# The attention half's up-projection in seven-product units, its gate scaled earlier, the halves added in DRAM

## The chip, the cores and the metric

One core of a Trainium2 chip runs the whole kernel in one launch. The metric is device time in microseconds (us). The engines are TensorE (PE; its weight loads are PEld), VectorE (DVE), ScalarE (ACT), GpSimd (POOL) and SyncE (SP, which only issues DMAs here). Each engine works through its own queue in order.

## The reference, cut to what matters

The input is a residual stream x of 512 tokens by 2048 channels, and all arithmetic is float32.

```python
h = rmsnorm(x, attn_norm_g);  proj = h @ w_in        # u, v_sgu, q, k, v_att, g_a, g_b
y_a = chunked_spatial_gating(gelu(u), rmsnorm(gelu(v_sgu)))     # 512 x 1024
y_b = stick_breaking_attention(rmsnorm(q), rmsnorm(k), v_att)   # 512 x 1024
merged = sigmoid(g_a) * (y_a @ w_up_a) + sigmoid(g_b) * (y_b @ w_up_b)
x = x + merged @ w_o
x = x + (silu(gate) * up) @ w_ffn_out      # gate, up = rmsnorm(x) @ w_ffn_in
x = x + sigmoid(rmsnorm(x) @ w_ple_gate) * (p @ w_ple)
```

## The kernel before

Everything is kept transposed: channels lie on the 128 partitions, tokens along the free dimension. A **block** of an operand has 256 channels by 512 tokens (1024 columns of SBUF). A **pair** (`pair`, line 798) computes one block of 256 output channels. It consists of **units**, one for each 256 input channels.

A float32 product is made of three products of a high and a low part (`mm3`, line 287). A unit is of one of two kinds (`Pair.add`, line 648).

- Kind P, plain: 12 matmuls of 512 columns into two PSUM banks, y and z (lines 294 to 296).
- Kind S, Strassen's seven products on 256 x 256 quarters: undoubled it is 21 matmuls of 256 columns (lines 294 to 296) into four banks. Doubled, the high and low parts of the moving operand go through in one matmul of 512 columns (line 683). The quarters are put together by ACT and DVE in `mix` (lines 700 to 726) or `mix_doubled`.

Weights come two units at a time (a **double**). SP loads them into one of a few landing blocks, ACT splits off the high part (line 357) and DVE the low part (line 354). For an S double GpSimd also issues a DMA that adds two blocks onto the landed ones (line 361), and DVE makes two sums (line 373). There are three slots of split weights.

An operand is held as a **form**. A plain form (`plain_form`, line 604) is a block split into high and low. A late form (`late_form`, line 588) is what S units need: it loads a block, splits it (lines 284, 285) and can then serve as a plain operand. It later loads the same block again, the **second block**, and makes the other sums and splits of it (`plain_first`, line 525 for the sums). `until` says up to which pair j each unit still uses the plain operand, so that the first pairs of a stage are P while the second blocks are being worked on.

`tick()` (line 207) sets the order of this background work. It is called several times in each pair. It fetches a first block for one of the next three forms, builds the next form if its block has arrived and there is room, or else (`elif`) fetches one second block. A second block is held back as long as one of the next three forms of its stage has not been fetched. `after(n, fn)` puts work off by n ticks. Room comes from two arenas in SBUF: `parts` for forms, which has eight places for late forms, and `wholes` for raw blocks.

The stages in order are: the input projection with the attention and the spatial gating between its pairs (loop from line 1287), the **up stage** (loop from line 1338), the product with w_o (loop from line 1363), w_ffn_in, w_ffn_out in three passes, and the gate of the embeddings.

In the up stage j runs over eight output blocks, and for each j there is a pair "b" (y_b, attention) and then a pair "a" (y_a, spatial gating). All 16 pairs are PPPP. The gates' raw values were spilled to DRAM by the input projection. For each pair the gate block is loaded, DVE multiplies it by the row of the RMS norm (`scaled`, line 1209, 1212), ACT takes the sigmoid (line 1345), and DVE multiplies by the two banks (line 1350). After pair a, DVE adds the kept half b (line 1354), and one tick later SP stores the block `mix` (line 1332). The late forms of the w_o stage load it from there.

In the w_o stage the first pair (j = 0) is all P, the second is SSSSPPPP, the others are all S and doubled. At the end of a pair, `onto` adds the result to a block of x. Where a pair has both kinds, `rest` first takes in the banks y and z (line 787).

Of the kernel before, what the change touches and what calls it, by code (L numbers as in the profile page):

```python
# [31 lines left out]

PASSES = "SSSSSSSS", "SSSSSSSS", "SSSSPP"
# [35 lines left out]
def hybrid_layer(  # L69
# [137 lines left out]
    def tick():  # L207
# [396 lines left out]
    def plain_form(src, ready=always, gain=None, raw=1024, how="low", far=False):  # L604
        def steps(form):
            hi, lo = form.blocks = parts.take(1024, how), parts.take(1024, how)
# [16 lines left out]
        return Form("P", steps, [(parts, 1024, how)] * 2 + [(wholes, raw, "low")] * bool(raw),  # L623
# [555 lines left out]
    def sgu_v(rnd, o):  # L1179

        for h in range(2):
# [18 lines left out]
            for t in range(NT):  # L1200
# [7 lines left out]
                op0=ALU.mult, op1=ALU.add)  # L1208

# [70 lines left out]
    def y_form(c, i):  # L1280
        return plain_form((lambda: y_a[i]) if c == "a" else lambda: load(y_spill[i]),
                          lambda: len(y_done) == 8, raw=0 if c == "a" else 1024,
                          far=c == "b")

    ys = {(c, i): y_form(c, i) for c in "ba" for i in range(4)}
    build(ys.values())
    for n, ((w, i), pr) in enumerate(zip(order, made())):
# [25 lines left out]
        else:  # L1313
            d = tc.dram_tile([P, 1024], F32, name=nm("gsp"))
            nc.sync.dma_start(out=d, in_=o)
            gate_spill[w, i] = d
    finish_waiting()
    give(*att.values())


    part = {}
# [16 lines left out]
    for j in range(KU):  # L1338
        for b in "ba":
# [3 lines left out]
            def gate(g=g):  # L1343
                scaled(g, row1)
                nc.scalar.activation(g, g, AF.Sigmoid)

            after(1, gate)
            pr = pair([ys[b, i] for i in range(4)], last=j == KU - 1)
            for h, ps in zip((g[:, :T], g[:, T:]), pr.ends()):
                nc.vector.tensor_tensor(out=h, in0=h, in1=ps, op=ALU.mult)  # L1350
            if b == "b":
                part[j] = s
            else:
# [201 lines left out]
```

## Time and profile before

| | us |
|---|---|
| runs | 2667.51, 2673.37, 2673.16 (median 2673.16) |
| the profiled execution | 2668.2 |
| its span in the profile | 2666.5 |
| PE busy | 2640.4 |
| DVE busy | 2236.4 |
| ACT busy | 1413.9 |
| POOL busy | 453.4 |

The span is the time from the first to the last instruction of the program; the 1.7 us beside it lie around the program. Ends of matmuls are modelled, so PE's speed is read from the distance between starts, and from stretches with a known number of matmuls.

### The profile page before, as it was taken

How to read it: one execution, taken by the hardware profiler on the slowest of the kernel's cores; microseconds unless marked ns; L12 is line 12 of the kernel's file. 1: busy time of each engine (PE TensorE's matmuls, PEld its weight loads, DVE VectorE, ACT ScalarE, POOL GpSimd, SP SyncE). 2: the span in 40 equal slices, each digit the busy share in tenths (PEclk: the TensorE clock that was granted, in tenths of full speed). 3: DMA queues.
4: the chain of work that ended last, by engine and by line, in shares of the span. 5: the costliest groups of instructions: out<-in, count | busy, mean ns of one | idle time of the engine just before them, and what ended most of it. 6: DMA issues, size and time to landing. Idle time of an engine off the chain costs nothing.

```text
span 2666.5 us, 42598 instructions
## 1 busy us (share of the span) xinstructions
PE 2640.4 (99%) x15354; PEld 2312.4 (87%) x15354; DVE 2236.4 (84%) x3791; ACT 1413.9 (53%) x2245; POOL 453.4 (17%) x557
## 2 busy tenths in 40 slices
PE   8999999999999999999999999999999999999999
PEld 7888898888998888888888888888888888889898
DVE  8687878787887658989889888888889989989876
ACT  7656565655554334576444444444445445455643
POOL 0222322222220001101111111111110211211010
PEclk9999999999999999999999999999999999999999
DMA  7577777677775669988888878888787989988884
GB/s 227 158 190 174 185 173 187 171 182 197 179 188 186 214 212 264 239 265 223 220 218 207 210 194 207 203 203 202 197 209 223 263 220 277 226 248 246 252 229 134
DMA packets 293875, 560.16 MB, mean 210 GB/s; under 512 B 26400, under 2 KB 140832, under 8 KB 293664
## 3 DMA queue, kind: packets, MB, share of 16 engines
q1 hardware_dynamic: 231408, 442.08, 50.4%
q0 software_dynamic: 62256, 115.37, 27.0%
q8 instruction: 120, 1.97, 0.3%
q14 instruction: 91, 0.75, 0.1%
HBM read 505.97 MB, written 51.38 MB: 209 GB/s over the span
## 4 chain that ended last, share of the span: by engine, by line
PE 88%; DVE 5%; ACT 2%; DMA 2%; issue 1%; POOL 0%; SPq 0%; POOLq 0%; DVEq 0%; ACTq 0%
PE ps L683 49%; PE ps L295 10%; PE ps L296 10%; PE ps L294 10%; PE small L683 6%; DVE wlo L354 2%; DVE out L742 1%; PE small L1145 1%; PE small L1021 1%; DMA wholes<-x 1%; DMA wholes<-w_in 1%; ACT whi L357 1%; DVE wholes L373 0%; PE small L1095 0%; DVE parts L285 0%
## 5 line engine op out<-in xcount | busy, mean ns | idle before, releaser
L683 PE MATMUL ps<-parts,whi 128*128 128x512 f32 x4200 | 1404.7, 398 | 3.7 <-DVE out L787 3.1
L357 ACT ACTIVATE whi<-wholes 128x512 fp32r<-128x512 f32 (+3 forms) x941 | 872.5, 940 | 727.6 <-DVE wholes L373 270.5
L354 DVE TENSOR_TENSOR wlo<-wholes,whi 128x512 fp32r<-128x512 f32 (+3 forms) x941 | 982.7, 1079 | 65.8 <-ACT whi L357 64.0
L683 PEld LDWEIGHTS ps<-parts,wlo 128*128 128x128 f32 x4200 | 788.9, 188 | 178.4 <-DVE wlo L354 1.1
L683 PE MATMUL ps<-parts,wlo 128*128 128x256 f32 x4200 | 832.0, 279 | 0.0
L683 PEld LDWEIGHTS ps<-parts,whi 128*128 128x128 f32 x4200 | 676.4, 189 | 10.2 <-issue 4.5
L294 PE MATMUL ps<-parts,whi 128*128 128x256 f32 (+1 forms) x1822 | 598.9, 330 | 8.0 <-ACT parts L284 5.6
L295 PE MATMUL ps<-parts,whi 128*128 128x256 f32 (+1 forms) x1838 | 605.9, 330 | 0.8 <-DVE parts L285 0.8
L296 PE MATMUL ps<-parts,wlo 128*128 128x256 f32 (+1 forms) x1838 | 605.8, 330 | 0.0
L295 PEld LDWEIGHTS ps<-parts,whi 128*128 128x128 f32 x1838 | 348.4, 190 | 39.0 <-DVE parts L285 2.4
L294 PEld LDWEIGHTS ps<-parts,whi 128*128 128x128 f32 x1822 | 344.6, 190 | 41.5 <-ACT parts L284 6.7
L296 PEld LDWEIGHTS ps<-parts,wlo 128*128 128x128 f32 x1838 | 348.8, 190 | 30.8
L373 DVE TENSOR_TENSOR wholes<-wholes 128x256 f32<-128x256 f32 x822 | 345.1, 420 | 21.7 <-DMA wholes<-w_ffn_in 2.6
L742 DVE TENSOR_TENSOR out<-out,ps 128x256 f32<-128x256 f32 x490 | 202.9, 416 | 149.9 <-ACT out L739 149.4
L361 POOL DMA_DIRECT2D wholes<-w_ffn_in x170 | 148.0, 870 | 691.2 <-DVE wholes L373 197.4
L361 POOL DMA_DIRECT2D wholes<-w_in x132 | 116.3, 882 | 523.1 <-DMA wholes<-w_in 146.8
L683 PE MATMUL small<-parts,whi 128*128 128x512 f32 x480 | 190.3, 396 | 0.0
L285 DVE TENSOR_TENSOR parts<-wholes,parts 128x1024 fp32r<-128x1024 f32 (+3 forms) x148 | 138.1, 945 | 23.0 <-ACT parts L284 23.0
L284 ACT ACTIVATE parts<-wholes 128x1024 fp32r<-128x1024 f32 (+3 forms) x148 | 119.3, 830 | 55.1 <-DVE wholes L525 33.3
L739 ACT ACTIVATE out<-ps 128x256 f32<-128x256 f32 x258 | 95.7, 382 | 49.9 <-PE ps L683 46.4
L361 POOL DMA_DIRECT2D wholes<-w_ffn_out x64 | 55.6, 869 | 358.3 <-DMA wholes<-w_ffn_out 136.5
L1395 ACT ACTIVATE out<-out 128x512 f32<-128x512 f32 x44 | 27.9, 634 | 159.2 <-DVE out L1394 159.2
(123 smaller groups left out, 1750.2 us busy)
## 6 DMA issues: line engine op xcount, KB each, us to landing
wholes<-w_ffn_in SPq DMA_DIRECT2D x170, 384.0 KB, 5.6
wholes<-w_in SPq DMA_DIRECT2D x132, 384.0 KB, 5.0
wholes<-w_ffn_in SPq DMA_DIRECT2D x170, 256.0 KB, 4.8
wholes<-w_ffn_in POOLq DMA_DIRECT2D x170, 256.0 KB, 5.4
wholes<-w_in SPq DMA_DIRECT2D x132, 256.0 KB, 4.0
wholes<-w_in POOLq DMA_DIRECT2D x132, 256.0 KB, 5.0
wholes<-w_ffn_out SPq DMA_DIRECT2D x64, 384.0 KB, 6.3
wholes<-x SPq DMA_DIRECT2D x45, 512.0 KB, 5.6
```

The lines of the kernel that those rows point to most:

```text
L284: return (nc.scalar.activation(hi, src, AF.Copy), nc.vector.tensor_tensor(out=lo, in0=src, in1=hi.bitcast(F32), op=ALU.subtract))
L285: nc.vector.tensor_tensor(out=lo, in0=src, in1=hi.bitcast(F32), op=ALU.subtract))
L294: nc.tensor.matmul(ps, sh, mh, start=start, stop=False)
L295: nc.tensor.matmul(ps, sh, ml, start=False, stop=False)
L296: return nc.tensor.matmul(ps, sl, mh, start=False, stop=stop)
L354: in_turn(nc.vector.tensor_tensor(out=self.lo[:, blocks], in0=r, in1=h.bitcast(F32), op=ALU.subtract))
L357: in_turn(nc.scalar.activation(h, r, AF.Copy))
L361: nc.gpsimd.dma_start(out=raw[:, 3:5], in_=self.src[:, 1:3], accum_op=ALU.add)
L373: in_turn(nc.vector.tensor_tensor(out=o, in0=x, in1=y, op=ALU.add))
L683: m = nc.tensor.matmul(out, l, r, start=first and k == 0, stop=last and k == 1)
L739: in_turn(nc.scalar.activation(out, x, AF.Copy, scale=scale))
L742: in_turn(nc.vector.tensor_tensor(out=out, in0=x, in1=y, op=op))
```

## The change

- The pairs "a" and "b" change places: "a" comes first for each j.
- The forms of y_b become late forms. Pair b is PPPP for j = 0, SSPP for j = 1 and SSSS from j = 2 on (`UP_UNTIL`), undoubled, and ends with `mix` and one multiplication of 1024 columns.
- The gate block is multiplied by the norm's row in the input projection, two ticks after its pair, before it is spilled. The up stage only takes the sigmoid.
- The halves are no longer added by DVE. Pair a's product is stored by SP as `mix`, and pair b's product is added to it in DRAM by an accumulating DMA that GpSimd issues. Only then may the w_o stage load the block.
- `tick()` may fetch a second block in the same tick in which it builds a form, and also while first blocks are still to come, if `wholes` has room for these.
- In the w_o stage x's block is loaded at the start of its own pair, not a pair sooner. The norm's row and the attention's tiles are given back sooner. The first form of y_a takes its high part at the upper end of `parts`.

```diff
+UP_UNTIL = 1, 1, 2, 2
...
             builds.popleft().step()
-        elif seconds and fits([(wholes, 5 * 256, "old")]):
+        if seconds:
             f = (urgent or seconds)[0]
-            if f.used or not any(b.stage == f.stage and b.ready() and not b.there
-                                 for b in list(builds)[:AHEAD]):
+            first = [] if f.used else [b for b in list(builds)[:AHEAD]
+                                       if b.stage == f.stage and b.ready() and not b.there]
+            if fits([(wholes, 5 * 256, "old")] + [(wholes, 1024, "old") for _ in first]):
                 f.fetch_second()
...
+        if rnd == 3:
+            assert ("b", 3) in y_done
+            give(*att.values())
+            att.clear()
...
-            for b in "ba":
-                plan((w_up_a if b == "a" else w_up_b)[j], "PPPP")
+            for b in "ab":
+                plan((w_up_a if b == "a" else w_up_b)[j],
+                     "PPPP" if b == "a" else now("SSSS", UP_UNTIL, j))
...
+        if c == "a":
+            return plain_form(lambda: y_a[i], ready, raw=0, how="low" if i else ("high", "low"))
+        return late_form(lambda size=1024: load(y_spill[i], size), ready, far=True)
...
+            def spill_gate(o=o, d=d):
+                scaled(o, row1)
+                nc.sync.dma_start(out=d, in_=o)
+
+            after(2, spill_gate)
...
-            def gate(g=g):
-                scaled(g, row1)
-                nc.scalar.activation(g, g, AF.Sigmoid)
-
-            after(1, gate)
-            pr = pair([ys[b, i] for i in range(4)], last=j == KU - 1)
-            for h, ps in zip((g[:, :T], g[:, T:]), pr.ends()):
-                nc.vector.tensor_tensor(out=h, in0=h, in1=ps, op=ALU.mult)
-            if b == "b":
-                part[j] = s
+            after(1, lambda g=g: nc.scalar.activation(g, g, AF.Sigmoid))
+            pr = pair([ys[b, i] for i in range(4)], last=j == KU - 1, j=j,
+                      until=UP_UNTIL if b == "b" else None)
+            if pr.n["S"]:
+                tt(g, g, pr.out(), ALU.mult)
             else:
-                nc.vector.tensor_tensor(out=g, in0=g, in1=part[j].f(), op=ALU.add)
-                give(part.pop(j))
-                after(1, lambda j=j, s=s: store("mix", j, s))
+                for h, ps in zip((g[:, :T], g[:, T:]), pr.ends()):
+                    tt(h, h, ps, ALU.mult)
+
+            def store_merged(b=b, j=j, s=s):
+                if b == "a":
+                    nc.sync.dma_start(out=spill["mix", j], in_=s.f())
+                else:
+                    nc.gpsimd.dma_start(out=spill["mix", j], in_=s.f(), accum_op=ALU.add)
+                    there.add(("mix", j))
+                give(s)
+
+            after(1, store_merged)
...
-        if j < KU - 1:
-            raw.append(load(xT[j + 1]))
+        h = load(xT[j])
```

More of the change, by code (lines that the diff above doesn't have):

```diff
@@ L604, in plain_form @@
     def plain_form(src, ready=always, gain=None, raw=1024, how="low", far=False):
+        hows = [how] * 2 if isinstance(how, str) else how
         def steps(form):
-            hi, lo = form.blocks = parts.take(1024, how), parts.take(1024, how)
+            hi, lo = form.blocks = [parts.take(1024, h) for h in hows]
             w = form.raw()
@@ L621, in steps @@
             yield
-        return Form("P", steps, [(parts, 1024, how)] * 2 + [(wholes, raw, "low")] * bool(raw),
+        return Form("P", steps, [(parts, 1024, h) for h in hows] + [(wholes, raw, "low")] * bool(raw),
                     ready, src, far)
@@ L1280, in y_form, with ready @@
     def y_form(c, i):
[L1281 to L1285, printed above, removed]
+        def ready():
+            return len(y_done) == 8
+        if c == "a":
+            return plain_form(lambda: y_a[i], ready, raw=0, how="low" if i else ("high", "low"))
+        return late_form(lambda size=1024: load(y_spill[i], size), ready, far=True)
+    ys = {(c, i): y_form(c, i) for c in "ab" for i in range(4)}
     build(ys.values())
```

13 lines of the change are left out of this document (3 added, 10 removed).

## The prediction

> **What bounds the kernel now.** I read the page first, then the busy times by stage, then the rows of PE at the stage borders.
>
> ```profile
> span 2666.5 us, 42598 instructions
> PE 2640.4 (99%) x15354; PEld 2312.4 (87%) x15354; DVE 2236.4 (84%) x3791; ACT 1413.9 (53%) x2245; POOL 453.4 (17%) x557
> ```
>
> Busy times by stage (window; its length; PE, PEld, DVE, ACT, POOL busy; granted clock; DMA share; GB/s): input projection, up stage, start of w_o, most of w_ffn_in.
>
> ```profile
> 114.00:820.00 706.00, 698.21 (x4461) 623.12 (x4460) 576.31 (x1016) 423.37 (x868) 180.39 (x243) 1.00 0.72 182
> 820.00:995.00 175.00, 174.26 (x770) 143.53 (x769) 108.15 (x118) 64.36 (x63) 0.88 (x1) 1.00 0.61 205
> 995.00:1050.00 55.00, 51.91 (x277) 44.78 (x276) 44.34 (x74) 25.23 (x33) 6.94 (x8) 0.99 0.89 258
> 1190.00:1850.00 660.00, 659.51 (x3781) 575.41 (x3780) 589.94 (x1057) 329.32 (x460) 115.72 (x133) 1.00 0.82 211
> ```
>
> The reader is to see that PE is the bound nearly everywhere: in w_ffn_in it idles 0.5 us of 660 while DVE is busy 89%. In the up stage it idles 0.7 us, with DVE at 62%. So work taken from DVE there gives nothing by itself. Time can only come from fewer or shorter matmuls, or from the few places where PE stands. The change touches two such places. The first is early in the up stage:
>
> ```profile
> 832.10 0.73 PE L294 MATMUL ps<-parts,whi 128*128 128x512 f32 x2 [0.21 <-ACT parts L284]
> 833.36 0.50 PE L295 MATMUL ps<-parts,whi 128*128 128x512 f32 x1 [0.52 <-DVE parts L285]
> ```
>
> Here PE waits 0.21 and 0.52 us for the split of the y forms. The second is in w_o:
>
> ```profile
> 1043.65 0.63 PE L683 MATMUL ps<-parts,whi 128*128 128x512 f32 x2
> 1047.37 0.47 PE L683 MATMUL ps<-parts,whi 128*128 128x512 f32 x1 [3.09 <-DVE out L787]
> ...
> 1049.01 0.63 PE L683 MATMUL ps<-parts,wlo 128*128 128x256 f32 x2
> ```
>
> ```profile
> 1041.00:1043.90 2.90, 2.90 (x19) 2.49 (x17) 2.90 (x10) 1.08 (x2) 0.00 (x0) 1.00 1.08 232
> 1043.90:1047.40 3.50, 0.41 (x3) 0.06 (x1) 3.50 (x5) 1.00 (x3) 0.89 (x1) 1.00 0.91 331
> 1048.60:1052.10 3.50, 3.50 (x14) 3.02 (x13) 3.19 (x6) 2.74 (x3) 0.88 (x1) 0.51 1.00 277
> ```
>
> PE stands 3.1 us because `rest` (L787) of the second w_o pair is late on a DVE that is busy without a break. Then PE's granted clock is 0.51 for 3.5 us, which loses another 1.7 us. Both together are about 4.9 us, the largest single loss that I found in the trace.
>
> The Trainium skill bears on that price: "TensorE: Matmul & The Clock Gate", section "HAM oscillation — how this bites in real kernels", asks for no idle gaps of PE over about 3.4 us. By that rule 3.1 us would have stayed free of the half clock and the place would cost 3.1. The trace differs: 3.1 us of idleness was enough.
>
> **The matmuls.** One P unit runs from one start to the next start of the following unit; four undoubled S units fill a window of their own:
>
> ```profile
> 1015.28 0.39 PE L294 MATMUL ps<-parts,whi 128*128 128x512 f32 x1
> ...
> 1018.00 0.28 PE L294 MATMUL ps<-parts,whi 128*128 128x256 f32 x1
> ```
>
> ```profile
> 1018.00:1028.07 10.07, 10.07 (x85) 10.06 (x84) 9.07 (x15) 6.31 (x8) 0.89 (x1) 1.00 0.85 212
> ```
>
> A P unit takes 1018.00 - 1015.28 = 2.72 us. An S unit takes 10.07 / 4 = 2.518 us (84 matmuls of 0.12 us). The seven products save an eighth of the columns, but a 256-column matmul is a little dearer per column, so a unit saves 0.20 us, or 7.4%. S units are 2 in pair j = 1 and 4 in each of j = 2 to 7: 26. **26 x 0.204 = 5.3 us** on PE, the bound. This is the surest term.
>
> **DVE in the up stage.** Prices are from before's groups:
>
> ```profile
> L354 DVE TENSOR_TENSOR wlo<-wholes,whi 128x1280 fp32r<-128x1280 f32 x26 | 38.6, 1486 | 5.2 <-ACT whi L357 5.2
> L354 DVE TENSOR_TENSOR wlo<-wholes,whi 128x512 fp32r<-128x512 f32 x26 | 17.8, 684 | 3.8 <-ACT whi L357 3.8
> L373 DVE TENSOR_TENSOR wholes<-wholes 128x256 f32<-128x256 f32 x50 | 21.0, 420 | 2.3 <-DMA wholes<-w_ffn_out 1.6
> ```
>
> ```profile
> L354 DVE TENSOR_TENSOR wlo<-wholes,whi 128x1024 fp32r<-128x1024 f32 x33 | 40.3, 1222 | 12.9 <-ACT whi L357 12.9
> L1350 DVE TENSOR_TENSOR wholes<-wholes,ps 128x512 f32<-128x512 f32 x30 | 20.2, 686 | 18.1 <-PE ps L296 17.2 <-ACT wholes L1345 1.0
> L1212 DVE TENSOR_TENSOR wholes<-wholes 128x1024 f32<-128x1024 f32 x16 | 19.6, 1223 | 26.1 <-DMA wholes<-gsp 26.1
> L1354 DVE TENSOR_TENSOR wholes<-wholes 128x1024 f32<-128x1024 f32 x7 | 8.6, 1225 | 0.2
> L284 ACT ACTIVATE parts<-wholes 128x1024 fp32r<-128x1024 f32 x11 | 11.4, 1051 | 14.0 <-DMA wholes<-mix 8.3 <-DMA wholes<-y 5.6
> L285 DVE TENSOR_TENSOR parts<-wholes,parts 128x768 fp32r<-128x768 f32 x3 | 2.9, 952 | 0.0
> ```
>
> Removed: 16 scalings, 19.6 us, and 8 additions of halves, 9.8 us. Added: an S double costs DVE 1.49 + 0.68 + 2 x 0.42 = 3.01 instead of 1.22, so 13 doubles cost 23.3 more. Six `mix` cost 5 x 0.42 + 0.69 = 2.8 each, 16.8, and that of j = 1 costs 3.1. The second blocks of four y_b forms cost 4 x 0.42 + 0.95 = 2.6 each, 10.5. Sum: 108.2 - 29.4 + 53.7, about 132 of 170 us, or 78%. That is below the 89% at which w_ffn_in loses nothing, so I cost it at nothing. Its cover is thin in one place: a pair b of S units needs 6.0 + 2.8 + 1.2 = 10.0 us of DVE in 10.07 us of PE. The pair a beside it needs only 3.8 in 10.9, and split weights are one double (5 us) ahead.
>
> **The start of the up stage.** In before the y_b blocks must come from DRAM in the last pair of the projection. With y_a first, the forms needed first are already in SBUF, and y_b has one pair more. I take the 0.7 us above as gone (bounds 0 and 0.7).
>
> **The gate's scaling in the projection.** 16 operations of 1.22 us go onto DVE, which goes there from 576 to 596 of 706 us. They are put off two ticks, and behind each on DVE stand the steps of the attention, for which PE waits at places like this:
>
> ```profile
> 288.98 1.42 PE L1145 MATMUL small<-wholes 128*128 128x512 f32 x3 [0.84 <-ACT wholes L1138]
> ```
>
> From below, nothing excludes a loss of 0. From above, each of some 12 gates beside the attention delays PE by 0.4 us, 5 us in all. I take **1.5 us** lost, nearer to 0, since most of that DVE's work isn't waited for. The buffer of the gate is used again only two pairs later, and its store moves with it.
>
> **The halves added by DMA.** Half b no longer goes through DVE but through a GpSimd DMA, and the load of the merged block waits on SP until that has landed. The same form of DMA stands in w_ffn_out (issues: KB each, median us from issue to landing; then its minimum, median and maximum):
>
> ```profile
> x<-out POOLq DMA_DIRECT2D x16, 512.0 KB, 8.9
> wholes<-mix SPq DMA_DIRECT2D x16, 512.0 KB, 5.5
> ```
>
> ```profile
> DMA to landing us min/median/max: 5.0/8.9/9.7
> ```
>
> For blocks 0 to 6 there are a pair or more of time, and nothing is lost. SP stands some 5 us longer per block, and behind the load stand weights (a slot and a landing ahead, over 10 us) and the next gate block, whose sigmoid ACT can wait for at 37% busy. Block 7 is the last operand of the first w_o pair. Before:
>
> ```profile
> 998.41 0.33 SPq L1332 DMA_DIRECT2D mix<-wholes  x1
> ...
> 1001.83 0.33 SPq L516 DMA_DIRECT2D wholes<-mix  x1
> ```
>
> ```profile
> 1010.41 1.22 DVE L285 TENSOR_TENSOR parts<-wholes,parts 128x1024 fp32r<-128x1024 f32 x1
> ```
>
> ```profile
> 1000.38 0.87 POOL L361 DMA_DIRECT2D wholes<-w_o  x1 [6.37 <-DMA wholes<-w_o]
> ```
>
> Store at 998.4, load at 1001.8, split done by 1011.6, and needed at 1015.28, the start of the last unit: 3.7 us to spare. By durations alone the split could end at 1001.83 + 5.5 + 1.05 (ACT, L284) + 1.22 = 1009.6, so 5.7 to spare. The adding DMA takes 8.9 where the store took 3.4, 5.5 more: 0.2 to spare. It can also stand on POOL behind a w_o weight's addition that starts at 1000.38 and takes 0.87 (2.8 us), and behind a DVE that is up to 2 us late after an S pair. Bounds: 0 (landing in 5.0 us) and 4.6 of standing plus 1.7 of half clock, 6.3. I take **2.0 us** lost.
>
> **Second blocks sooner.** Busy time of DVE in the sums of second blocks (L525) around the start of w_o:
>
> ```profile
> 860.00:920.00 60.00, 4.54 (x12) 1.00 0.58 192
> 920.00:995.00 75.00, 0.00 (x0) 1.00 0.63 214
> 995.00:1015.00 20.00, 0.00 (x0) 1.00 0.90 277
> 1015.00:1050.00 35.00, 7.64 (x19) 0.98 0.88 248
> ```
>
> Three forms get their second blocks in the up stage (12 operations), none from 920 to 1015, and five crowd behind 1015. These are what makes L787 late. Fetching in the same tick as a build brings them forward into DVE's idle time. Against it: late forms of y_b take more of `parts` than plain ones, so only two merged forms fit beside them, not three. One more second block, 2.6 us of DVE, comes to this place; and loads behind block 7's stand on SP until its addition has landed. Bounds: nothing and the whole 4.9 us. I take **3.5 us** won.
>
> x's block in w_o is loaded a pair later but 20 us before its use, against the 5.5 us that a load of this size takes in the row of mix above: nothing. In the other stages PE hardly stands, so sooner second blocks give nothing there.
>
> **Sum.** -5.3 - 0.7 + 1.5 + 2.0 - 3.5 = -6.0 us. On the profiled execution, 2668.2, that is 2662.2. The shown runs lie at 2667.5 and at 2673.2 and 2673.4, so the profiled one is of the lower kind and 5 us under the median. I take the middle of the two kinds, 2670.5, and forecast **2664.5 us**.
>
> **The rivals.**
>
> 1. Everything hides: block 7 in time, the 4.9 us wholly gone, the scaling free: -5.3 - 0.7 - 4.9 = -10.9, 2659.6. For it: 7.6 us of idle DVE between 995 and 1018. Against it: the tight block 7.
> 2. Block 7 late at its upper bound and the stall at 1044 still there, since second blocks queue behind it on SP: -5.3 - 0.7 + 1.5 + 6.3 = +1.8, 2672. For it: 8.9 against 3.4 us. Against it: 5.7 us to spare.
> 3. Slower: DVE becomes the bound of the S pairs. From j = 2 on it needs 10.0 of 10.07 us and in some of them a merged form as well (1.22 + 2.6). If PE then waits for split weights 3.7 us in each of six pairs, that is +22 - 6 = +16, 2686. It decides from the point where DVE's backlog passes the 5 us that weights are ahead. 3.8 doesn't, and pair a pays it back, so I hold it unlikely.
> 4. The change doesn't do what it says: no room in `wholes`, second blocks come when they came. Then -6.0 + 3.5 = -2.5, 2668.
>
> **How the numbers follow.** Chances: forecast 0.45, rival 1 0.18, rival 2 0.17, rival 3 0.10, rival 4 0.10. Against the median of 2673.16, 0.3%, about what a measurement can tell from no change, is 8 us, so faster means under 2665.1. Rival 1 and half of the forecast lie there: 0.40. Slower is rival 3 and a little of rival 2: 0.12. The rest is 0.48. The range reaches from rival 1 on a run of the lower kind, 2668.2 - 10.9 = 2657, to rival 2 with the scaling at 5 us on a run of the upper kind, 2673.2 + 5.3 = 2678. It leaves out rival 3.
>
> **What would show it.** The up stage 6 us shorter with PE idle under 1 us in it; no stall at L787 in the second w_o pair, or a shorter one, with no half clock; a wait of the last unit of the first w_o pair for L285 or L284 of 0 to 4 us; L525 busy between 995 and 1015; losses of PE in the projection up by 1 or 2 us. A wait of PE for L354 in the S pairs would prove rival 3.

## The result and the profile after

The changed kernel is slower: 2681.36 us (median of 6 runs, 2679.03 to 2686.46) against 2669.97 us for the kernel before on the same chip (6 runs, 2667.51 to 2673.37). The ratio is 1.0043, interval 1.0033 to 1.0053. That is some 11 us, and 3 us above the upper end of the range. The profiled execution took 2680.76 us, 12.6 more than that of before.

Line numbers below are those of the changed kernel unless a listing is of another: the three matmuls of a unit are L296 to L298, the doubled ones L687, the splits of forms L286 and L287, those of weights L359 and L356, GpSimd's addition of weights L363, DVE's sums L375, sums of second blocks L527 (the same helper line also holds the multiplications by the gate now), every plain load L518, `rest` L791, the sigmoid L1357, the store of pair a's product L1368, the addition of pair b's L1370. The page begins:

```profile
span 2678.6 us, 43332 instructions
PE 2640.7 (99%) x15589; PEld 2321.8 (87%) x15589; DVE 2268.5 (85%) x3893; ACT 1436.2 (54%) x2286; POOL 466.2 (17%) x578
```

The same four windows as before, with the columns of the prediction:

```profile
114.00:820.00 706.00, 701.02 (x4468) 625.31 (x4468) 594.92 (x1036) 429.25 (x871) 173.94 (x242) 1.00 0.73 185
820.00:995.00 175.00, 170.10 (x998) 151.40 (x997) 113.58 (x171) 74.25 (x88) 17.66 (x20) 0.98 0.86 250
995.00:1050.00 55.00, 48.17 (x242) 40.37 (x240) 48.39 (x80) 27.46 (x37) 7.09 (x9) 0.94 0.89 265
1190.00:1850.00 660.00, 656.12 (x3745) 571.61 (x3744) 583.94 (x1046) 327.65 (x457) 115.00 (x132) 1.00 0.83 209
```

The projection is no worse. PE now stands 4.9 us in the up stage (0.7 before), 6.8 in the start of w_o (3.1) and 3.9 in the window of w_ffn_in (0.5). In the up stage and w_o the granted clock is lower too, and the DMA share of the up stage went from 0.61 to 0.86. I follow the first stall backwards. PE, then DVE, ACT, SP and POOL (start, length, engine, line, idle time before and what ended it):

```profile
907.62 0.39 PE L297 MATMUL ps<-parts,whi 128*128 128x512 f32 x1
912.91 0.79 PE L298 MATMUL ps<-parts,wlo 128*128 128x512 f32 x1 [4.90 <-DVE wlo L356]
```

```profile
911.29 0.42 DVE L713 TENSOR_TENSOR out<-out 128x256 f32<-128x256 f32 x1 [11.26 <-ACT out L710]
911.64 1.22 DVE L356 TENSOR_TENSOR wlo<-wholes,whi 128x1024 fp32r<-128x1024 f32 x1
```

```profile
909.72 1.06 ACT L1357 ACTIVATE wholes<-wholes 128x1024 f32<-128x1024 f32 x1 [11.86 <-DMA wholes<-gsp]
910.68 1.07 ACT L710 ACTIVATE out<-ps 128x512 f32<-128x512 f32 x2
```

```profile
901.17 0.33 SPq L518 DMA_DIRECT2D wholes<-mix  x1
901.54 0.43 SPq L518 DMA_DIRECT2D wholes<-gsp  x1
```

```profile
894.02 0.89 POOL L1370 DMA_DIRECT2D mix<-wholes  x1 [7.74 <-DVE wholes L527]
```

The reader is to see one queue after another stop behind a DMA. GpSimd issues the addition of a block at 894.02. SP's next instruction loads that merged block, so SP stands until the addition has landed, at 901.15. Behind it in SP's queue is the next gate block, issued at 901.54 and landed at 909.70. ACT's next instruction is that block's sigmoid: ACT idles 11.86 us, 3.7 of them before the load is issued and 8.2 while it is under way. The copies of `mix` (L710) behind it could have run: the last matmul of their S pair starts at 901.81. DVE idles 11.26 us behind those copies, and the low part of the weights that PE wants comes after them. PE's row names DVE L356 as the releaser, but DVE was not busy, it was waiting. Then the clock is low (window 910.60 to 917.40):

```profile
910.60:917.40 6.80, 4.49 (x11) 3.52 (x12) 5.93 (x11) 2.55 (x5) 0.29 (x1) 0.50 0.51 175
```

This stall costs 5.1 us of standing and 2.2 of half clock, 7.3 in all, found from the starts. It is the deepest of a kind, as the waits in 840 to 1010 us show (engine, line, what it waited for: us in total, times, longest). The changed kernel's ACT and SP:

```profile
ACT wholes L1357 <- DMA wholes<-gsp: 46.3, 12, 11.9
ACT whi L359 <- DMA wholes<-w_up_b: 12.1, 3, 5.6
...
SPq L518 <- DMA mix<-wholes: 75.7, 13, 8.9
```

SP in the kernel before, same window:

```profile
SPq L516 <- DVE wholes L1354: 24.6, 7, 4.9
...
SPq L516 <- DMA mix<-wholes: 15.9, 8, 2.2
```

The second place is the start of w_o:

```profile
1006.42 0.50 PE L297 MATMUL ps<-parts,whi 128*128 128x512 f32 x1 [1.96 <-DVE parts L287]
...
1016.49 1.43 PE L296 MATMUL ps<-parts,whi 128*128 128x512 f32 x3 [4.25 <-ACT parts L286]
```

```profile
1002.22 0.87 POOL L363 DMA_DIRECT2D wholes<-w_o  x1 [5.77 <-DMA wholes<-w_o]
1002.85 1.16 POOL L1370 DMA_DIRECT2D mix<-wholes  x1
```

```profile
1011.75 1.28 SPq L518 DMA_DIRECT2D wholes<-mix  x3
...
1015.38 1.06 ACT L286 ACTIVATE parts<-wholes 128x1024 fp32r<-128x1024 f32 x1 [7.19 <-DMA wholes<-mix]
```

Block 7's addition starts at 1002.85 (its store started at 998.41 before) behind a w_o weight on POOL. SP can load the block at 1011.75, ACT splits it at 1015.38, and PE has stood 4.25 us. With a smaller wait before it, a later one of 0.6 us and a half clock from 1016.4 to 1023.2, PE loses 10.8 us here. The kernel before lost 4.9 here, in its stall at L787, which is absent now. The third place is the border to w_ffn_in:

```profile
1203.18 0.86 PE L296 MATMUL ps<-parts,whi 128*128 128x512 f32 x3 [2.78 <-ACT parts L286]
```

```profile
1204.10:1207.50 3.40, 3.40 (x13) 2.92 (x12) 3.40 (x9) 3.04 (x6) 1.03 (x2) 0.51 0.99 225
```

By stages, from the ends of the same operations in both traces, the changed kernel is 2.8 us behind at the end of w_o's seventh pair, loses 5.5 more by early w_ffn_in, 0.1 in the rest of that stage, 2.6 by the end of the first 14 pairs of w_ffn_out and 1.3 in what follows. So some 9 of the 12 us in the profiled executions are lost behind w_o's seventh pair.

### The profile page after: what moved, and what is told of

Its sections match the earlier page's. It is cut to its first block, busy times and chain, and to the rows that moved or that the text cites. A ratio compares the mean times of both kernels' runs of the same rounds, so it can differ in the third digit from the quotient of the medians.

```text
span 2678.6 us, 43332 instructions
## 1 busy us (share of the span) xinstructions
PE 2640.7 (99%) x15589; PEld 2321.8 (87%) x15589; DVE 2268.5 (85%) x3893; ACT 1436.2 (54%) x2286; POOL 466.2 (17%) x578
## 5 line engine op out<-in xcount | busy, mean ns | idle before, releaser
L687 PE MATMUL ps<-parts,whi 128*128 128x512 f32 x4200 | 1404.0, 398 | 2.2 <-DVE out L746 1.0
L359 ACT ACTIVATE whi<-wholes 128x512 fp32r<-128x512 f32 (+2 forms) x954 | 882.9, 939 | 715.5 <-DVE wholes L375 306.5
L356 DVE TENSOR_TENSOR wlo<-wholes,whi 128x512 fp32r<-128x512 f32 (+2 forms) x954 | 992.1, 1074 | 40.1 <-ACT whi L359 39.7
L687 PEld LDWEIGHTS ps<-parts,wlo 128*128 128x128 f32 x4200 | 789.0, 188 | 179.0 <-issue 1.9
L687 PE MATMUL ps<-parts,wlo 128*128 128x256 f32 x4200 | 832.7, 279 | 0.0
L687 PEld LDWEIGHTS ps<-parts,whi 128*128 128x128 f32 x4200 | 675.4, 189 | 10.3 <-issue 4.4
L298 PE MATMUL ps<-parts,wlo 128*128 128x256 f32 (+1 forms) x1916 | 619.0, 324 | 6.7 <-DVE wlo L356 6.7
L297 PE MATMUL ps<-parts,whi 128*128 128x256 f32 (+1 forms) x1916 | 619.7, 324 | 5.8 <-DVE parts L287 5.8
L296 PE MATMUL ps<-parts,whi 128*128 128x256 f32 (+1 forms) x1899 | 611.2, 323 | 14.0 <-ACT parts L286 12.1
L297 PEld LDWEIGHTS ps<-parts,whi 128*128 128x128 f32 x1916 | 365.1, 191 | 41.4 <-DVE parts L287 8.6
L296 PEld LDWEIGHTS ps<-parts,whi 128*128 128x128 f32 x1899 | 362.0, 191 | 43.3 <-ACT parts L286 12.7
L298 PEld LDWEIGHTS ps<-parts,wlo 128*128 128x128 f32 x1916 | 365.4, 191 | 35.7 <-DVE wlo L356 8.3
L375 DVE TENSOR_TENSOR wholes<-wholes 128x256 f32<-128x256 f32 (+1 forms) x848 | 355.0, 419 | 28.3 <-DMA wholes<-w_ffn_in 4.5
L363 POOL DMA_DIRECT2D wholes<-w_ffn_in x170 | 148.2, 871 | 698.5 <-DVE wholes L375 225.4
L363 POOL DMA_DIRECT2D wholes<-w_in x132 | 116.0, 879 | 532.2 <-DMA wholes<-w_in 144.1
L687 PE MATMUL small<-parts,whi 128*128 128x512 f32 x480 | 190.4, 397 | 0.0
L287 DVE TENSOR_TENSOR parts<-wholes,parts 128x1024 fp32r<-128x1024 f32 (+3 forms) x162 | 144.0, 900 | 28.6 <-ACT parts L286 28.5
L286 ACT ACTIVATE parts<-wholes 128x1024 fp32r<-128x1024 f32 (+3 forms) x162 | 124.9, 795 | 60.5 <-DVE wholes L527 34.2
L363 POOL DMA_DIRECT2D wholes<-w_ffn_out x64 | 55.7, 871 | 354.4 <-DMA wholes<-w_ffn_out 135.7
```

The source lines that it names most:

```text
L286: return (nc.scalar.activation(hi, src, AF.Copy), nc.vector.tensor_tensor(out=lo, in0=src, in1=hi.bitcast(F32), op=ALU.subtract))
L287: nc.vector.tensor_tensor(out=lo, in0=src, in1=hi.bitcast(F32), op=ALU.subtract))
L296: nc.tensor.matmul(ps, sh, mh, start=start, stop=False)
L297: nc.tensor.matmul(ps, sh, ml, start=False, stop=False)
L298: return nc.tensor.matmul(ps, sl, mh, start=False, stop=stop)
L356: in_turn(nc.vector.tensor_tensor(out=self.lo[:, blocks], in0=r, in1=h.bitcast(F32), op=ALU.subtract))
```

## The experiments

Each ratio is to the kernel before in runs on the same chip, in five rounds. The profiled execution of one kernel can lie 3 us or more off its median, so medians carry the verdicts and traces the causes. In the changed kernel the last gate block is scaled after the place of the norm's row has been handed on. In e4 that place is overwritten by then, so there the block is scaled by other data. From e5 on (not in e15) the row is kept three ticks longer.

**e1: the old rule for second blocks, alone.**

```diff
-        if seconds:
+        elif seconds and fits([(wholes, 5 * 256, "old")]):
```

> The changed kernel with the old rule for second blocks (one piece of background work a tick, held back while a first block is to come). Theory A: the new rule itself costs the stalls at the start of w_ffn_in (span 1200, 5.4 us with the half clock) and at the start of w_ffn_out (span 2059, 3 us), because second blocks get in front of the last first block; with the old rule both go, and the span falls from 2678.6 by 8 to 12 us. Rival B: these stalls come from what the earlier stages hand over late, not from the rule; then they stay and the span falls by less than 2 us.

1.0037 [1.0024, 1.0049]. The up stage still has a stall (4.7 us at 887.7, ended by a split of weights) and ACT still waits 44.2 us for gate blocks. At the border the stall stays, though it comes 9 us later. So the rule by itself isn't the cause, as rival B had it.

**e2: the new rule alone, in the kernel before** (the same lines the other way round).

> The kernel before with the new rule for second blocks and nothing else. Theory A: +5.4 and +3 us at the two later stage borders, and at most 4.9 us won at span 1044: 2666.5 becomes 2668 to 2675. Rival B: no loss at the borders, 4.9 us won: 2662.

1.0024 [1.0015, 1.0033]. The part that I priced at -3.5 us costs 6 by itself. The stall at L787 is gone from the trace, but PE stands 3.1 us at 1013.3 for the split of a form (L285, 1.6 more at 1017.5), and 3.0 at 1178.6 for a copy (L874). The profiled span, 2674.4 us, lies in theory A's range.

**e3: the halves added by DVE, as before.**

```diff
+            if b == "a":
+                part[j] = s
+            else:
+                nc.vector.tensor_tensor(out=g, in0=g, in1=part[j].f(), op=ALU.add)
+                give(part.pop(j))
+                after(1, lambda j=j, s=s: store("mix", j, s))
```

> The changed kernel with the halves added by VectorE and one store again, instead of a store and an adding DMA; all else changed. Theory A: the adding DMA lands late, SP stands before the load of the merged block and the next gate block stands behind it, so the stalls at span 907 (7.3 us with the half clock) and of the last unit of the first w_o pair (about 6 us of the 10.8 at span 1004 to 1018) go: -9 to -13 us. Rival B: the up stage's DMA engines are simply too full (share about 0.9, 0.61 before) and the order on SP hardly matters: the stalls stay, -3 us at most.

1.0064 [1.005, 1.0077]: slower still. The kept half takes room and DVE 9.8 us. There are stalls of 2.3 and 1.9 us at 911 and 936, and 2.5 us at L791. The DMA share of the up stage is 0.70, and SP stands only 20.5 us on mix transfers (840 to 1010 us), yet ACT still waits 46.4 us for gate blocks. So putting the addition back is no cure, and gate blocks come late without the adding DMA too.

**e4: plain units in pair b, all else as changed.**

```diff
-                     "PPPP" if b == "a" else now("SSSS", UP_UNTIL, j))
+                     "PPPP")
...
-        return late_form(lambda size=1024: load(y_spill[i], size), ready, far=True)
+        return plain_form(lambda: load(y_spill[i]), ready, raw=1024, far=True)
```

> The changed kernel with plain units and plain forms in pair b, all else changed. It shows what the S units give and cost. Theory A: the 5.3 us on TensorE come back and the stall at span 907 stays about as it is, since it hangs on the adding DMA: 2678.6 + 5 = 2684. Rival B: S weights and second blocks fill the DMA engines and make the stalls at span 907 and 1004: these go with them, 2678.6 + 5.3 - 10 = 2674.

1.0032 [1.0019, 1.0045]. Its up stage has no loss at all, while SP stands on the mix DMAs nearly as long as in the changed kernel. ACT's sigmoid hardly waits. ACT, then SP:

```profile
ACT wholes L1357 <- DMA wholes<-gsp: 5.0, 5, 3.4
...
SPq L518 <- DMA mix<-wholes: 68.6, 15, 8.7
```

```profile
820.00:995.00 175.00, 175.00 (x780) 145.22 (x779) 82.05 (x97) 62.05 (x62) 7.00 (x8) 1.00 0.75 228
```

So the wait of SP isn't a price in itself. It becomes one when S pairs bring more transfers and more split weights that stand behind a late sigmoid. At the end of w_o's seventh pair e4 is 3.5 us ahead of before, but by early w_ffn_in it is 3.0 behind: PE stands 4.7 us at the border, and half clock follows. So the stalls go, as rival B had it, but the time, 2679.78, doesn't fall to its 2674.

**e5: the gate block loaded one pair sooner.**

```diff
+    turns = [(b, j) for j in range(KU) for b in "ab"]
+    gate_blocks = deque([load(gate_spill[turns[0]], 1024, "low")])
...
-            s = load(gate_spill[b, j], 1024, "low")
+            if turns.index((b, j)) + 1 < len(turns):
+                gate_blocks.append(load(gate_spill[turns[turns.index((b, j)) + 1]], 1024, "low"))
+            s = gate_blocks.popleft()
```

> The changed kernel with each gate block loaded one pair sooner, so that on SP it stands in front of the load of the merged block (the norm's row is also kept until the last gate block is scaled, which touches no time). Theory A: the sigmoid's wait for the gate block is what stops ScalarE, then VectorE, then TensorE in the S pairs; the stall at span 907 (7.3 us) goes, ScalarE's wait for gate blocks in the up stage falls from 40.5 to under 5 us, and the forms of w_o get built sooner: span 2678.6 - 8 to 10. Rival B: the DMA engines are too full in the up stage (share 0.86, 0.62 before); the blocks are late wherever they stand: -2 us at most.

1.0032 [1.002, 1.0044]. The stall at 907 is gone, and so is ACT's wait for gate blocks, but the wait only moved: SP stands 88.8 us on the mix DMAs, and now the weights behind it are late. The ratio falls by 0.11%, with overlapping intervals, where theory A had 8 to 10 us.

```profile
ACT whi L359 <- DMA wholes<-w_up_b: 40.7, 9, 11.8
```

In e5's trace a gate block is loaded at 970.44, right after the addition out of the place it goes to landed at 970.42, and the weights follow at 970.87.

**e6: e5 with the old rule and x's block one pair sooner, as before the change.**

```diff
+    raw = deque([load(xT[0])])
...
-        h = load(xT[j])
+        if j < KU - 1:
+            raw.append(load(xT[j + 1]))
```

> As the run before, and with the old rule for second blocks and x's block loaded a pair sooner again in w_o. Theory C: the losses at the later borders come from second blocks that are fetched in front of the last first block as soon as wholes has room; a fuller wholes and the old rule give before's order back, so the borders at w_ffn_in (5.4 us) and w_ffn_out (3 us) lose as little as before: 2661 to 2665. Rival D: they come from another placing of blocks or from lateness handed on, and stay at 4 to 8 us: 2669 to 2673.

0.9996 [0.9984, 1.0007]: level with before, 2668.99 us, so short of theory C's 2661 to 2665. Against before the border now loses 0.8 us, where it lost 5.5.

**e7: e4's plain units with the old rule and x's block sooner**, gate blocks as in the changed kernel.

> Plain units and plain forms in pair b, the old rule, x's block a pair sooner: what is left of the change is the order of the pairs, the scaling in the projection and the adding DMA. Theory C: the up stage and w_o end 3 to 4 us sooner than before (as with plain units and the new rule) and the later borders are as before: 2663. Rival D: 2668 to 2672.

0.998 [0.997, 0.9991], faster than both kernels. The median, 2665.53, lies between the two forecasts. What is left of the change here is mainly the order of the pairs, the scaling in the projection and the addition by DMA.

**e8: only block 7's halves added by DVE** (and the row kept).

```diff
+            if j == KU - 1 and b == "a":
+                held = s
+                continue
+            if j == KU - 1:
+                tt(g, g, held.f(), ALU.add)
+                give(held)
+                after(1, lambda j=j, s=s: store("mix", j, s))
+                continue
```

> The changed kernel with the last merged block alone (j = 7) added by VectorE and stored once. Theory A: the adding DMA of block 7 lands 5 us later than a store would, and the last unit of the first w_o pair waits for it: 4.4 us, and about 2 of half clock, go: -5 to -7 us. Rival: VectorE is so far behind there that the addition on it costs the same: 0 to -2 us.

1.0033 [1.0022, 1.0043]. The 4.25 us wait becomes one of 1.3, but a stall of 3.5 us at L791 takes its place at 1046.85. The start of w_o has two candidates for the last arrival, block 7 and DVE's backlog, and removing the one lets the other show. The time falls by 0.10% against the changed kernel, where theory A had 5 to 7 us; the intervals overlap.

**e9: e6, with both waits of SP taken away:** a gate block goes where the oldest free room is, and the merged block's load is ordered 4 ticks later.

```diff
-                gate_blocks.append(load(gate_spill[turns[turns.index((b, j)) + 1]], 1024, "low"))
+                gate_blocks.append(load(gate_spill[turns[turns.index((b, j)) + 1]]))
...
-                    there.add(("mix", j))
+                    after(4 if j < KU - 1 else 0, lambda j=j: there.add(("mix", j)))
```

> The kernel of e6 (all of the change but the rule: the second blocks go by the rule of before; gate blocks and x's block are loaded one pair sooner) with two edits that take SyncE off the waits for the mix DMAs: a gate block is put where the oldest free room is instead of into the place of the gate block that the mix transfer still reads, and the load of a merged block is ordered 4 ticks later, when its addition has landed. Theory (SyncE, standing on mix DMAs for some 76 to 89 us of the up stage, brings the Strassen pairs' weights late): SyncE's wait on the mix DMAs falls under 20 us, the wait of ScalarE's splits for w_up_b's weights falls from 40 us to under 15, up stage and start of w_o lose 3 to 6 us less, and the time is 2662 to 2666. Rival (VectorE's additions for the Strassen forms are what comes late at the start of w_o, whoever loads them): the DMA waits of SyncE go but the losses of TensorE do not, and the time stays at 2669 within 1.5 us. Second rival (the addition by DMA is slow because the DMA engines are full): the wait moves from SyncE to the first operand of w_o, and the time is 2672 or more.

0.999 [0.9982, 0.9999], median 2668.45, so short of the theory's 2662 to 2666. The expected fall of SP's wait failed: it is still 80.0 us. ACT's wait for w_up_b did fall, from 27.0 to 13.2 us, and the up stage up to 995 us loses nothing. What counts is which loads stand behind the wait, not its sum.

**e10: all S units, e9's loads, the new rule in attention's half only**, x's block a pair sooner from its third on.

```diff
-        if seconds:
+        if seconds and (seconds[0].stage < 2 or not stepped):
```

> The changed kernel with all its Strassen units, with gate blocks a pair sooner and SyncE freed as in e9, with the new rule for second blocks only in the y and mix operands (attention's half), the rule of before in the later stages, and x's block a pair sooner from its third on. Theory (the new rule costs only at the later borders, and takes away the stall of 3.3 us in the w_o stage where it is kept): the later borders stand as in e6 (within 1 us of before), and the stall near 1044 us of before is absent; 2658 to 2664. Rival (the new rule crowds the start of w_o also where the loads are free): w_o's front stands 4 us or more over before, and the time is 2669 to 2675.

0.9996 [0.9987, 1.0004], 2669.66. The profiled execution was 10 us ahead of before at the end of w_o's seventh pair and gave half of that back later. At 2663.31 us it is the fastest of eleven; the median is level with before and above the theory's 2658 to 2664.

**e11: plain units with e10's rule and x's block**, gate blocks as in the changed kernel.

> As e10 but with plain units in the second half's up-projection as before and no Strassen forms there, so that of the change there stay the scaling in the projection, the order of the pairs, the halves added by DMA, and the new rule in attention's half alone. Gate blocks are loaded as in the changed kernel. Theory (the front of e4, 3.5 us ahead of before at the end of w_o's seventh pair, goes with the later borders of e7, 0.5 us behind before in sum): 2661 to 2665. Rival (what is gained in front is given back at the norm of attention's output, where the weights and second blocks are on time anyway): 2665 to 2668, as e7.

1.0012 [1.0003, 1.0021], 2673.59: worse than both expectations. In its trace 2.7 us are lost again by early w_ffn_in and 4.8 at the end of the kernel. I can't name the cause.

**e12: e11 with e9's gate blocks.**

> As e11, with the gate blocks a pair sooner and put where the oldest free room is. With plain units TensorE lost nothing in the up stage of e4 although SyncE stood on the mix DMAs there too, so theory (SyncE's waits cost only where Strassen pairs want split weights): same as e11 within 1.5 us. Rival (SyncE's waits cost in any form of the pairs): 2 to 4 us under e11. The difference of e10 and e12 is the price of the Strassen units with SyncE freed: TensorE saves 5.3 us in them; by the theory that VectorE is their cost e10 is 2 us or more over e12, by the theory that late loads are, e10 is 3 to 5 us under e12.

0.9984 [0.9976, 0.9993], 2666.76. It beats e11 by 0.28%, so here the place and time of the gate loads are worth something in plain pairs too; under the old rule (e7, e16 below) that doesn't repeat. Against e12, e10 with S units and a later merged load is 0.12% behind, with overlapping intervals: I see no gain from the S units here, though they save 5.3 us, 0.2%, on PE.

**e13: the changed kernel with only e9's loads** (gate blocks sooner and in other room, merged load later). Rule and x's block are as changed.

> The changed kernel with the new rule everywhere and x's block at its own pair, and only SyncE freed as in e9: gate blocks a pair sooner and put where the oldest free room is, the load of a merged block 4 ticks after its addition. Theory (what the change lost in the up stage and at the start of w_o is SyncE standing on the mix DMAs, and the rest is lost at the border to w_ffn_in by rule and x's block): the front goes from 2.8 us behind before to 6 us or more ahead of it, the border stays 4 us or more behind, and the time is 2671 to 2676. Rival (the front is gained only where rule and x's block are undone as well, since they crowd the room of the same blocks): the front stays within 3 us of before, and the time is 2678 to 2681.

0.9987 [0.9979, 0.9996], 2667.41. From 1.0043 to 0.9987 is 0.56%, 15 us: more than the whole slowdown, and better than either forecast. All arithmetic of the change is still there. SP still stands 67.5 us on mix transfers. ACT's waits for DMAs, and PE by window:

```profile
ACT whi L359 <- DMA wholes<-w_up_b: 13.1, 4, 6.2
ACT parts L286 <- DMA wholes<-mix: 3.7, 1, 3.7
ACT whi L359 <- DMA wholes<-gsp: 3.3, 1, 3.3
```

```profile
820.00:995.00 175.00, 175.00 (x1032) 156.08 (x1031) 126.60 (x188) 83.39 (x96) 20.17 (x23) 1.00 0.89 265
995.00:1050.00 55.00, 51.05 (x264) 43.65 (x263) 45.68 (x76) 27.59 (x35) 6.25 (x8) 0.94 0.93 279
```

PE does not stand in the up stage, with the DMA share even higher than in the changed kernel (0.89 against 0.86). A gate block even takes longer to land in 840 to 1010 us (median 8.0 us, 5.4 in the changed kernel, 3.7 in the kernel before), but PE waits for nothing up to 995 us. So the traffic by itself doesn't make PE stand; when the loads are ordered, and into what place, decides. Against before the border loses 1.8 us, with rule and x's block as changed, where I expected 4 or more: most of the loss there too went away with the loads.

**e14: the other half: old rule and x's block sooner, gate loads as changed** (and the row kept).

> The changed kernel with the rule of before and x's block loaded a pair sooner as before, gate blocks and SyncE's order as in the changed kernel. It stands between e1 (rule of before alone, 1.0037) and e6 (gates a pair sooner too, 0.9996). Theory (the border to w_ffn_in wants x's block sooner; the up stage wants the gate blocks sooner): the border is within 1.5 us of before, the stall of the up stage is there as in e1, and the time is 2673 to 2677. Rival (the up stage is what costs, and x's block does nothing): as e1, 2680.

1.0055 [1.0044, 1.0067]: outside both expectations and slower than e1. ACT waits 43.5 us for gate blocks again, there are stalls at 889 and 1020 as in e1, and the start of w_o loses 13.8 us where e1 lost 8.5. So what made e6 level is e5's gate loads together with these two edits, not these two alone.

**e15: x's block at its own pair, in the kernel before.**

```diff
-    raw = deque([load(xT[0])])
     for j in range(KU):
-        if j < KU - 1:
-            raw.append(load(xT[j + 1]))
+        h = load(xT[j])
```

> The kernel before with one part of the change alone: x's block of the w_o stage is loaded at its own pair instead of one pair ahead. The forecast put that at nothing. Theory (its load then stands at the border behind second blocks and norm work, which is where e1 lost 4.8 us): 2 to 5 us slower than before, with the first split of the next stage's last block later after the last square. Rival (x's block has 20 us of room in w_o, the forecast's step): within 1 us of before.

1.0011 [1.0002, 1.002]: 3 us, which I had priced at nothing. In the trace not the border but the stall of before is longer, 4.76 us where it was 3.09 (line as in the kernel before):

```profile
1050.06 0.47 PE L683 MATMUL ps<-parts,whi 128*128 128x512 f32 x1 [4.76 <-DVE out L787]
```

**e16: e7 with e9's gate blocks.**

> e7 (plain units, rule of before, x's block a pair sooner: 0.998) with gate blocks a pair sooner and put where the oldest free room is. Theory (with plain units the waits of SyncE cost TensorE nothing): as e7 within 1.5 us, 2664 to 2667. Rival (they cost in any form): 2660 to 2663, the quickest of all. Against e9 it also prices the Strassen units under the rule of before: theory that VectorE's backlog takes what TensorE saves, e9 is level or behind by up to 3 us.

0.9993 [0.9985, 1.0002], 2668.57; the intervals of e7 and e16 overlap. e9, the same loads with S units (and a later merged load), is at 0.999: level.

**e17 and e18: e13's two edits apart, each on e5.**

> e5 (gate blocks a pair sooner) with one of the two further edits of e13 alone: a gate block is put where the oldest free room is, not into the place that the mix transfer still reads. e5 stands at 1.0032 and e13, with both edits, at 0.9987. Theory (the place is what counts: the wait for the mix transfer then no longer stands ahead of a gate block and the split pairs' weights behind it): 0.9987 to 1.0005, and ScalarE waits for w_up_b under 20 us where e5 has 40.7. Rival (the early order of the merged block's load is what counts, since SyncE stands there until the addition has landed): as e5, 1.002 or more.

> e5 with the other edit of e13 alone: the load of a merged block is ordered 4 ticks after its addition was issued, not 1. Theory (the place of the gate blocks counts): as e5, 1.002 or more, and ScalarE still waits some 30 to 40 us for w_up_b. Rival (the order of the merged block's load counts): 0.9987 to 1.0005. If both e17 and e18 stay at 1.002 or more, only both waits taken away together help.

e17 1.0003 [0.9994, 1.0012], e18 1.0016 [1.0007, 1.0024]. e17 lies in its theory's range, but ACT waits 26.8 us for w_up_b there, not under 20; e18 lies between its two forecasts, with 21.6 us (40.7 in e5, 13.1 in e13). So neither theory alone holds: each edit gives part. From the changed kernel down: the gate block sooner -0.11% (e5), its other room -0.29% (e17), the merged load later -0.16% (e18). The first is within the noise. Their sum, -0.56%, is that of e13; with intervals of 0.1% to either side, so close a match is partly luck.

## Why the prediction was wrong, point by point

**Halves added by DMA: the step that failed.** It said that for blocks 0 to 6 nothing is lost, since behind SP's longer stand there are weights over 10 us ahead and a gate block that ACT can wait for at 37% busy. The average of ACT hid what matters: its queue is in order. Behind the sigmoid stand the copies of `mix`, which only S pairs have, and the splits of weights, two for an S double where a P double has one. I counted SP's stand as 5 us for a block; it rose from 15.9 to 75.7 us, because a mix transfer can be waited for twice: by the merged block's load, and by the gate block that is loaded into its place. In the trace above, the load at 901.17 waits for the addition of 894.02, and the gate block at 912.69 for the store of 902.49 out of its place, landed at 912.68. Nor did I count the S doubles' extra loads, which raised the DMA share. A store of pair a's product took a median of 10.1 us to land (840 to 1020 us), against the 3.4 of block 7's store in the prediction's rows and the 6.5 that are the median of that kernel's eight stores of merged blocks:

```profile
mix<-wholes POOLq DMA_DIRECT2D x8, 512.0 KB, 6.2
mix<-wholes SPq DMA_DIRECT2D x7, 512.0 KB, 10.1
```

The longer stand of SP is only one way to make the sigmoid late, as e3 shows. What failed is that a late sigmoid is free: in the kernel before DVE waited 26.1 us for the same blocks and only plain pairs stood behind it: PE idled 0.7 us in the whole up stage. In the changed kernel it stood 4.9 us at 907.

For block 7 the landing (8.9 us), the place on POOL and the wait were as the upper bound had them: 4.25 us of standing against 4.6. The value taken, 2.0, was too near to zero, and the half clock around it lasted 6.8 us, where that bound counted 1.7 us of loss for one of 3.5.

**The S units: size right, gain not there.** Four units take 10.07 us in the changed kernel too:

```profile
941.13:951.20 10.07, 10.07 (x85) 10.06 (x84) 4.42 (x5) 3.23 (x4) 0.90 (x1) 1.00 0.87 239
```

The 5.3 us are saved on PE. But with the loads repaired, the S units are level with plain ones (e9, e16) or 0.12% behind (e10, e12). The traces show where part of it goes: at the start of w_o e13 and e9 lose 7.8 and 4.5 us, e12 1.8.

**Rival 3** forecast slower for another reason, DVE as the bound. DVE's load was estimated well: 132 us of 170, while e13 shows 126.6 of 175 with PE never idle. My mark for rival 3, a wait of PE for the low weights, did appear and would have misled: the releaser was an idle DVE.

**Second blocks sooner** were priced at -3.5, and they hardly came sooner. L527 has to be read by shapes in the changed kernel, since rows with `ps` or `out` are multiplications by the gate. DVE in 920 to 1015 us, then in 1015 to 1050:

```profile
L527 DVE TENSOR_TENSOR wholes<-wholes,ps 128x512 f32<-128x512 f32 x8 | 5.1, 680 | 0.0
L527 DVE TENSOR_TENSOR wholes<-wholes,out 128x1024 f32<-128x1024 f32 x4 | 4.9, 1217 | 0.0
L527 DVE TENSOR_TENSOR wholes<-wholes 128x256 f32<-128x256 f32 x4 | 1.5, 419 | 0.0
```

```profile
L527 DVE TENSOR_TENSOR wholes<-wholes 128x256 f32<-128x256 f32 x18 | 6.8, 418 | 5.2 <-DMA wholes<-mix 5.2
L527 DVE TENSOR_TENSOR wholes<-wholes 128x512 f32<-128x512 f32 x1 | 0.7, 685 | 0.0
```

Only four sums, those of one block, fall between 920 and 1015, where there were none, and all four come after 995; behind 1015 there are 19 as before. Up to 920 there are 24, but the four y_b forms take 16 of them. The other eight are of two merged blocks, where the kernel before had three; the prediction had said so ("only two merged forms fit") and still took 3.5 us as won. So DVE's idle time between 920 and 995 was not used, and the crowd behind 1015 stayed. The stall is absent in the changed kernel, where PE is late anyway; in e13, where PE is on time, it is back, and the clock halves around it:

```profile
1042.84 0.76 PE L687 MATMUL ps<-parts,whi 128*128 128x512 f32 x1 [2.65 <-DVE out L791]
```

```profile
1042.10:1048.90 6.80, 6.06 (x19) 5.23 (x20) 5.44 (x9) 2.74 (x3) 0.93 (x2) 0.50 0.94 275
```

Alone the rule costs 6 us (e2), though there too one block's four sums come before 1015. That sooner second blocks "give nothing" in the other stages left out that they can cost: e2's trace loses 3.7 us between w_o's seventh pair and early w_ffn_in. They may take room and queue from first blocks; no run shows that.

**x's block later** was priced at nothing and costs 3 us in the kernel before (e15).

**Right were** the start of the up stage (all of the 4.9 us that PE stands in its window is the stall at 907, so the 0.7 are gone) and DVE in the projection (594.9 us, forecast 596). The loss of 1.5 there was not seen: PE stands 5.0 us in that window, 7.8 before.

**What stays open.** Why the borders after w_o lose more in the changed kernel (e13 shows that most of that loss goes with the loads, not by which path), by which path e15 lengthens the stall at L787, and why e11 and e14 came out slower than expected. The parts don't add: the rule costs 6 us in the kernel before, and little beside e13's loads (e13 with it 0.9987, e9 without 0.999). The room in the arenas is shared, and I did not follow it block by block.

## What to carry to other kernels

When a wait is lengthened on an engine that only issues loads, write down the next loads behind it, and for each the instruction that waits for it on its in-order engine, and what stands behind that; a mean busy share says nothing about it. A buffer that a store or an addition still reads is not free: a load into it is a wait, and loading it sooner without other room only hands the wait to the next load. A releaser named in the profile is the cause only if it was busy before; if it was idle, ask what it waited for.

## What the runs showed of the hardware

The prediction took 3.1 us of idle PE as enough for the half clock, from one place. The traces show that the length of the idle time alone doesn't decide. In e3 2.09 us (from 911.8) were followed by 3.4 us at a granted clock of 0.50; 2.65 us in e13 by 6.8 us, shown above; 2.78 us in the changed kernel at 1203 by 3.4, and its 4.25 and 4.90 us by 6.8. But 2.62 us in the changed kernel (from 2059.4), 3.06 in e16 (from 1047.1) and 3.48 in e7 (from 645.1) were followed by none. The row of e3, then that of e7, whose 3.48 idle us lie in a window of full clock:

```profile
914.90:918.30 3.40, 3.40 (x9) 2.64 (x8) 3.29 (x7) 0.19 (x1) 0.00 (x0) 0.50 0.43 148
645.00:660.00 15.00, 11.52 (x79) 10.52 (x78) 9.39 (x18) 7.74 (x20) 5.55 (x6) 1.00 0.63 143
```

So these runs give no threshold between 2.1 and 3.5 us; the low stretches named here last 3.4 us or twice that. The Trainium skill ("TensorE: Matmul & The Clock Gate", section "HAM oscillation — how this bites in real kernels") asks only for gaps under about 3.4 us; here 2.09 and 2.65 us were too long, and 3.48 once was not.
